# Recurrent branch: arithmetic taken from GpSimd, drive and scan a pair behind, S5 rounding and one gate moved

## The chip, the cores and the metric

One core of one Trainium2 chip. The metric is device time in microseconds of one execution. Its engines are named here as in the profile: PE (TensorE's products) and PEld (its weight loads), DVE (VectorE), ACT (ScalarE), POOL (GpSimd), SP (SyncE, which only issues DMA here; ScalarE issues some too). The kernel before takes 1066.37 us, the median of 3 runs (1065.94 to 1066.80).

## The reference, cut to what matters

One layer of a backbone over 128 prompt and 512 sample tokens of 1024 channels, in fp32. `hn` is the normed and modulated input. Two branches come from it and are merged by sigmoid gates; an FFN follows.

```python
z = hn @ p["w_in"]
xa, ga, xs = split(z)                       # 1024, 1024 and 512 channels
u  = dwconv(xa, conv_w, conv_b)             # width 4 along the tokens
for d in (forward, backward):               # the recurrent branch (RG-LRU)
    r, i = sigmoid(u @ w_r[d] + b_r[d]), sigmoid(u @ w_i[d] + b_i[d])   # blocks of 64 channels
    log_a = -8 * r * softplus(-lambda[d])
    h[d] = scan(a = exp(log_a), b = sqrt(-expm1(2 * log_a)) * (i * u))
ya = gelu(ga) * (h[0] + h[1])
vs = gelu(S5(xs) + d * xs);  ys = vs * sigmoid(vs @ s5_w_glu + s5_b_glu)
gate_a, gate_b = split(sigmoid(hn @ w_gate + b_gate))
m  = (gate_a * (ya @ w_proj_lru) + gate_b * (ys @ w_proj_s5)) @ w_out
x  = x + g1 * rmsnorm(m);  then the FFN
```

## The kernel before

**Tiles.** Channels lie on partitions, tokens along the free axis, so a tile is 128 channels by 640 tokens, or by 644 to 648 where the prompt and the sample have borders for the convolution. The 1024 channels of the recurrent branch are 8 chunks `c`.

**Precision.** Every fp32 operand of a product is split in two halves of type fp32r: `hi` is the operand rounded, `lo` what is left, and a product is hi by hi, lo by hi and hi by lo. So each operand needs a rounding and a subtraction ahead of TensorE. For weights, `split_next` (L124) takes the next of the list `units`: ScalarE rounds `raw` to `wh`, VectorE subtracts to `wl`. The list is also the order in which SP loads the 512 KB of a unit, into four `raw` buffers; a load can start when the fourth unit before it is split. `use` (L153) makes a unit and, with `ahead=2`, the two behind it ready. For activations the pairs are `uh`, `ul` (from `u`, the convolution's output), `vsh`, `vsl` (from the S5 output `vs`), `ysh`, `ysl` (from the gated S5 output `yf`), and `yah`, `yal` (from a finished chunk of the branch).

**Order.** Nothing is scheduled by a planner: each engine executes its instructions in the order in which the code writes them, and waits on others by semaphores. PSUM has four buffers of one output tile each, so a product needs that the fourth tile before it has been read. SBUF tiles come from two pools, `tp` (20 tiles) and `lp` (27).

**The S5 end.** The last of four `vs` tiles is made by GELUs in `y_out` (L1019); a loop over `ct` (L1205) splits them, and `glu_job` (L1214) multiplies with `w_glu`, takes the sigmoid and multiplies with `vs`.

**The recurrent branch** is written as functions of a chunk: `lru_xa` (product), `lru_x` (copy of the product out of PSUM with a bias, borders set by GpSimd), `lru_conv` (four passes of VectorE and the rounding `uh`), `lru_ul`, `lru_w` (split of the small block weights), `lru_gates` (four products r and i of both directions, their sigmoids on ScalarE, `i` times `u` on GpSimd), `lru_ga` and `lru_gelu` (the GELU gate), `lru_decay` (tanh, exp and sqrt of a pair of chunks on ScalarE, a table load ahead of each kind), `lru_drive` (on VectorE (1 + a) times `ta`, on GpSimd times i·u; called the driving term below), `lru_scan` (two directions of prompt and sample, 128 and 512 columns each; two copies of the final state and the sum of directions on GpSimd) and `lru_finish` (times the GELU, split into `yah`, `yal`). The sigmoid's table is loaded ahead by `warm`.

The loop at L1231 goes over the pairs c = 2, 4, 6. A pass projects and convolves the chunks c and c+1, makes gates, decay and driving terms of c-2 and c-1, and scans and finishes c-4 and c-3. The last pass also rounds the S5 output `ys`. Behind the loop (L1281 on) come the gates of chunks 6 and 7, the scans 4 and 5, the last GELUs, decay, driving terms and scans of 6 and 7, and eight `ps5_job`s: the product of `ys` with `w_proj_s5`, and on VectorE its product with a mixing gate. The 16 mixing gates were made early (`gate_job`, L762) and all but one written to DRAM (`gd`); `gate_load` (L1267) reads such a gate tile back with a DMA that is issued from ScalarE's queue (`gld`). The 16th is made here, behind scan 7. Then q_pl, the eight products of `ya` with `w_proj_lru` (L1337 on), needs all eight `yah`, `yal`, and the output projection and the FFN follow.

## Time and profile before

| | |
|---|---|
| median of 3 runs | 1066.37 us (1065.94 to 1066.80) |
| the profiled execution, its own time | 1066.57 us |
| its span, first to last instruction | 1064.8 us |
| PE busy | 1001.6 us, 94% |
| PEld busy | 917.2 us, 86% |
| DVE busy | 714.2 us, 67% |
| ACT busy | 441.0 us, 41% |
| POOL busy | 301.1 us, 28% |
| bytes moved by DMA | 124.92 MB |
| chain that ended last, by engine | PE 66%, DVE 27%, issue 3%, DMA 2%, ACT 2% |

The shares are averages over stages with different limits. The S5 end runs until about 319 us, the recurrent branch from there to 488.83, where the first q_pl product starts; the projections and the FFN take the rest. Matmuls are pipelined with modelled ends, so a busy PE is not PE at its peak.

### The profile page before, as it was taken

Reading aid. Unit: us, or ns where it says so; the run is one execution under the profiler, and the core shown is the slowest. Engines: PE = TensorE matmul, PEld = TensorE weight load, DVE = VectorE, ACT = ScalarE, POOL = GpSimd, SP = SyncE. Lnnn points to the kernel's source line nnn. Section 1 sums busy time; section 2 is a strip of 40 time slices with the busy share of each in tenths; the row PEclk is TensorE's granted clock in tenths of the full one; section 3 lists DMA queues with packets and bytes.
Section 4 is the critical chain, followed back from the end, with each engine's and each line's share of the span. In section 5 each row is a group of like instructions: output and inputs, shape, how many; then the busy total and the mean of one; then the engine's idle time right before and its main releaser. Section 6 shows DMA issues by size and latency. Waiting matters only on the chain.

```text
span 1064.8 us, 16738 instructions
## 1 busy us (share of the span) xinstructions
PE 1001.6 (94%) x6615; PEld 917.2 (86%) x6615; DVE 714.2 (67%) x1127; ACT 441.0 (41%) x704; POOL 301.1 (28%) x248
## 2 busy tenths in 40 slices
PE   5998999989999998689999996999999999999997
PEld 3697888889999888588888886999999999888885
DVE  5689999983489999996346687555565565444114
ACT  5533332324439566741133325444444445333112
POOL 4000000000016665841220094555555452000002
PEclk9899999989999998899999998999999999999999
DMA  9774268624212220345656222232223332531202
GB/s 308 239 177 109 78 172 244 196 86 123 61 43 77 60 70 21 106 141 183 200 208 214 86 80 60 81 92 87 80 80 87 93 95 91 193 117 60 79 20 99
DMA packets 137134, 124.92 MB, mean 117 GB/s; under 512 B 17272, under 2 KB 115848, under 8 KB 137056
## 3 DMA queue, kind: packets, MB, share of 16 engines
q1 hardware_dynamic: 130384, 111.82, 34.5%
q10 hardware_dynamic: 6096, 11.90, 3.3%
q8 instruction: 52, 0.85, 0.3%
q0 software_dynamic: 576, 0.13, 0.1%
q14 instruction: 26, 0.21, 0.1%
HBM read 111.31 MB, written 12.53 MB: 116 GB/s over the span
## 4 chain that ended last, share of the span: by engine, by line
PE 66%; DVE 27%; issue 3%; DMA 2%; ACT 2%; SPq 0%; DVEq 0%; ACTq 0%
PE f L65 14%; PE ffX L65 13%; PE ffY L65 7%; PE q_pl L65 5%; PE q_wo L65 5%; PE q_ga L65 4%; DVE wl L59 3%; PE ffZ L65 3%; DVE F L59 3%; DVE hh L1156 3%; DVE sc L59 3%; PE q_g L65 2%; PE q_xa L65 2%; PE q_y L65 2%; PE q_xs L65 2%
## 5 line engine op out<-in xcount | busy, mean ns | idle before, releaser
L59 DVE TENSOR_TENSOR wl<-raw,wh 128x1024 fp32r<-128x1024 f32 x100 | 129.7, 1304 | 118.1 <-ACT wh L62 118.1
L62 ACT ACTIVATE wh<-raw 128x1024 fp32r<-128x1024 f32 x104 | 109.0, 1055 | 171.7 <-PE f L65 81.8
L59 DVE TENSOR_TENSOR wl<-s,wh 128x1024 fp32r<-128x1024 f32 x40 | 58.2, 1456 | 61.6 <-ACT wh L62 61.6
L65 PE MATMUL f<-wh,al 128*128 128x512 f32 x220 | 87.0, 396 | 0.0
L65 PE MATMUL f<-wl,ah 128*128 128x512 f32 x220 | 87.0, 396 | 0.0
L65 PE MATMUL f<-wh,ah 128*128 128x512 f32 x220 | 87.0, 395 | 0.0
L59 POOL TENSOR_TENSOR s<-raw 128x512 f32<-128x512 f32 x40 | 55.8, 1396 | 56.0 <-DVE wl L59 29.6
L997 POOL MEMSET Hst<- 128x8 f32 x4 | 0.4, 111 | 233.1 <-DMA Kd<-kt 181.7
L65 PE MATMUL q_g<-hnh,wh 128*128 128x320 f32 (+1 forms) x256 | 61.8, 323 | 3.1 <-DVE modT L59 3.1
L65 PE MATMUL q_g<-hnl,wh 128*128 128x320 f32 (+1 forms) x256 | 60.2, 317 | 0.0
L65 PE MATMUL q_g<-hnh,wl 128*128 128x320 f32 (+1 forms) x256 | 59.6, 315 | 0.0
L65 PEld LDWEIGHTS q_g<-hnh,wh 128*128 128x128 f32 x256 | 44.1, 196 | 8.5 <-ACT shift L62 5.0
L65 PEld LDWEIGHTS f<-wh,al 128*128 128x128 f32 x220 | 41.4, 188 | 9.9
L65 PEld LDWEIGHTS f<-wh,ah 128*128 128x128 f32 x220 | 41.4, 188 | 9.9
L65 PEld LDWEIGHTS f<-wl,ah 128*128 128x128 f32 x220 | 41.4, 188 | 9.9
L65 PE MATMUL ffX<-Th,wh 128*128 128x320 f32 x160 | 49.4, 309 | 0.0
L65 PE MATMUL ffX<-Th,wl 128*128 128x320 f32 x160 | 49.4, 309 | 0.0
L65 PE MATMUL ffX<-Tl,wh 128*128 128x320 f32 x160 | 49.4, 309 | 0.0
L59 POOL TENSOR_TENSOR x1b<-fo,x1b 128x512 f32<-128x512 f32 x4 | 6.9, 1722 | 149.2 <-DVE fo L1685 149.2
L62 ACT ACTIVATE u<-ffX 128x320 f32<-128x320 f32 x40 | 17.5, 437 | 67.6 <-PE ffX L65 67.6
L65 PEld LDWEIGHTS q_g<-hnl,wh 128*128 128x128 f32 x256 | 44.6, 195 | 0.0
L65 PEld LDWEIGHTS q_g<-hnh,wl 128*128 128x128 f32 x256 | 44.5, 194 | 0.0
(380 smaller groups left out, 3008.2 us busy)
## 6 DMA issues: line engine op xcount, KB each, us to landing
raw<-in_w_ff_in SPq DMA_DIRECT2D x44, 512.0 KB
raw<-in_w_mod SPq DMA_DIRECT2D x32, 512.0 KB
raw<-in_w_ff_out SPq DMA_DIRECT2D x22, 512.0 KB
raw<-in_w_in SPq DMA_DIRECT2D x20, 512.0 KB
wm<-in_w_mod SPq DMA_DIRECT2D x16, 512.0 KB
raw<-in_w_gate SPq DMA_DIRECT2D x16, 512.0 KB
gd<-gate ACTq DMA_DIRECT2D x15, 320.0 KB
gld<-gd ACTq DMA_DIRECT2D x15, 320.0 KB
```

The costliest lines, as they stand in the source:

```text
L59: (eng or DVE).tensor_tensor(out=out, in0=a, in1=b, op=op)
L62: ACT.activation(out=out, in_=in_, func=func, **kw)
L65: PE.matmul(out, lhsT=lhsT, rhs=rhs, start=start, stop=stop, skip_group_check=True)
L997: POOL.memset(hv[:, :, :, 16:17], 0.0)
L1156: DVE.tensor_tensor_scan(out=ov, data0=av, data1=bv, initial=ini, op0=ALU.mult, op1=ALU.add)
```

## The change

- **GpSimd's arithmetic.** In the recurrent branch and behind it, all products, sums, copies and low halves of GpSimd go to VectorE: i·u (now `lru_iu`, L1122), the second factor of the driving term, the sum of directions, the state copies, `ul`, two weights' `wl` and some `yal`. GpSimd keeps the memsets of the borders, and from q_pl on the sums of the mixed branches.
- **Roundings.** The high halves `uh`, `yah`, `ysh`, `vsh` and the copies of `xa` out of PSUM go from VectorE to ScalarE.
- **Order of a pass.** Driving terms and scans of a pair run in the next pass, between its two `lru_xa`; the products i·u, the splits of `u` and of the block weights and the second `lru_ga` stand between tanh and exp (`middle`), the next weight's split between exp and sqrt. `low` holds back the subtraction of `yal`.
- **The end.** The S5 output `ys` is split behind the gates of 6 and 7. The 16th mixing gate is made ahead of all `ps5_job`s, and its weight stands ahead of all `w_proj_s5` in the list of units. The loads of gate tiles 8 to 15 are issued behind the last GELUs, which stand behind the decay of 6 and 7.

`lru_decay(cs, between, then)`, unchanged, calls `between` behind tanh and `then` behind exp.

```diff
+    U_G.append(unit(colmajor(w_gate, GO[15] * 128), (128, KD, 128)))
     U_PS = [unit(w_ps5[:, m * 256:m * 256 + 256].rearrange("(k p) c -> p k c", p=128), (128, 4, 256))
-            for m in range(2)]
-    U_G.append(unit(colmajor(w_gate, GO[15] * 128), (128, KD, 128)))
-    U_PS += [unit(w_ps5[:, m * 256:m * 256 + 256].rearrange("(k p) c -> p k c", p=128), (128, 4, 256))
-             for m in range(2, 4)]
...
-        b = shift(q, eng=DVE)
-        DVE.tensor_scalar(out=x[:, 2:130], in0=q[:, 192:320], scalar1=b[:, 0:1], scalar2=None, op0=ALU.add)
-        DVE.tensor_scalar(out=x[:, 133:645], in0=q[:, 320:832], scalar1=b[:, 1:2], scalar2=None, op0=ALU.add)
+        b = shift(q)
+        act(x[:, 2:130], q[:, 192:320], AF.Identity, bias=b[:, 0:1])
+        act(x[:, 133:645], q[:, 320:832], AF.Identity, bias=b[:, 1:2])
-        cw = lambda k: vec("conv_w", k * 8 + c)
-        DVE.tensor_scalar(out=u, in0=x[:, 0:644], scalar1=cw(0), scalar2=vec("conv_b", c),
+        DVE.tensor_scalar(out=u, in0=x[:, 0:644], scalar1=vec("conv_w", c), scalar2=vec("conv_b", c),
-            DVE.scalar_tensor_tensor(out=u, in0=x[:, k:k + 644], scalar=cw(k), in1=u, op0=ALU.mult, op1=ALU.add)
+            DVE.scalar_tensor_tensor(out=u, in0=x[:, k:k + 644], scalar=vec("conv_w", k * 8 + c), in1=u,
+                                     op0=ALU.mult, op1=ALU.add)
+        fr[c] = (u,)
+
+    def lru_ul(c):
+        u = fr[c][0]
-        DVE.tensor_copy(out=uh, in_=u)
-        fr[c] = (u, uh, ul)
-
-    def lru_ul(c):
-        u, uh, ul = fr[c][0:3]
-        tt(ul, u, uh, ALU.subtract, POOL)
+        act(uh, u, AF.Copy)
+        tt(ul, u, uh, ALU.subtract)
+        fr[c] += (uh, ul)
...
     def lru_gates(c):
-        u, uh, ul, wh, wl = fr.pop(c)
+        u, uh, ul, wh, wl = fr[c]
...
+
+    def lru_iu(c):
+        u = fr.pop(c)[0]
+        for d in range(2):
+            tt(bk[c][d, 1], bk[c][d, 1], u, ALU.mult)
 
     def lru_decay(cs, between=None, then=None):
 
...
-    def lru_drive(ta, cs, eng=None):
+    def lru_drive(ta, cs):
-                tt(bk[c][d, 1], bk[c][d, 1], t, ALU.mult, eng or POOL)
-
-    def lru_scan(c, eng=None):
+                tt(bk[c][d, 1], bk[c][d, 1], t, ALU.mult)
+
+    def lru_scan(c):
...
-        (eng or POOL).tensor_copy(out=nl[:, 0, c:c + 1], in_=h[0][:, NP - 1:NP])
-        (eng or POOL).tensor_copy(out=nl[:, 1, c:c + 1], in_=h[1][:, 0:1])
+        DVE.tensor_copy(out=nl[:, 0, c:c + 1], in_=h[0][:, NP - 1:NP])
+        DVE.tensor_copy(out=nl[:, 1, c:c + 1], in_=h[1][:, 0:1])
-        tt(hf, hf, hb, ALU.add, eng or POOL)
+        tt(hf, hf, hb, ALU.add)
-    def lru_finish(c, eng=None):
+    def lru_finish(c):
+
-        DVE.tensor_copy(out=yh, in_=hf)
-        tt(yl, hf, yh, ALU.subtract, eng)
+        act(yh, hf, AF.Copy)
+        lows.append(lambda: tt(yl, hf, yh, ALU.subtract))
...
-        DVE.tensor_copy(out=vh, in_=v[:, 0:T])
+        act(vh, v[:, 0:T], AF.Copy)
...
+    ta = None
     for c in range(2, 8, 2):
-        xq = [lru_xa(c)]
-        if c > 2:
+        q = lru_xa(c)
+        if ta:
+            lru_drive(ta, (c - 4, c - 3))
             lru_scan(c - 4)
+        xs = [lru_x(c, q)]
+        q = lru_xa(c + 1)
+        if ta:
             lru_scan(c - 3)
-        xq.append(lru_xa(c + 1))
-        xs = [lru_x(c + j, xq[j]) for j in range(2)]
-        for j in range(2):
-            lru_conv(c + j, xs[j])
-            if c > 2:
-                lru_finish(c - 4 + j)
-        for j in range(2):
-            lru_gates(c - 2 + j)
-        for j in range(2):
-            lru_ul(c + j)
-            lru_w(c + j)
-        gq = [lru_ga(c), lru_ga(c + 1, ahead=1)]
-        ta = lru_decay((c - 2, c - 1))
-        lru_drive(ta, (c - 2, c - 1))
-        if c == 6:
-            use(U_PS[0], 0)
-            for m, g in enumerate(yf):
-                yh = ttile(f"ysh{m}", dt=F32R)[:, 0:T]
-                yl = ttile(f"ysl{m}", dt=F32R)[:, 0:T]
-                DVE.tensor_copy(out=yh, in_=g)
-                tt(yl, g, yh, ALU.subtract)
-                ys.append((yh, yl))
+        lru_conv(c, xs[0])
+        xs.append(lru_x(c + 1, q))
+        lru_gates(c - 2)
+        lru_gates(c - 1)
+        lru_conv(c + 1, xs[1])
+        gq = [lru_ga(c)]
+
+        def middle():
+            lru_iu(c - 2)
+            lru_iu(c - 1)
+            for j in range(2):
+                lru_ul(c + j)
+            for j in range(2):
+                lru_w(c + j)
+            gq.append(lru_ga(c + 1, ahead=1))
+
+        ta = lru_decay((c - 2, c - 1), middle, split_next)
+        if c == 4:
+            lru_finish(c - 4)
+            lru_finish(c - 3)
+            low()
         if c < 6:
             for j in range(2):
                 lru_gelu(c + j, gq[j])
...
+    gate_t[7] = gate_job(15, lp)
+    lru_drive(ta, (4, 5))
+    lru_iu(6)
+    lru_iu(7)
+    for m, g in enumerate(yf):
+        yh = ttile(f"ysh{m}", dt=F32R)[:, 0:T]
+        yl = ttile(f"ysl{m}", dt=F32R)[:, 0:T]
+        act(yh, g, AF.Copy)
+        tt(yl, g, yh, ALU.subtract)
+        ys.append((yh, yl))
     lru_scan(4)
+    ta = lru_decay((6, 7), lambda: [split_next(), lru_finish(2), lru_finish(3), low()])
     lru_scan(5)
     for j in range(2):
         lru_gelu(6 + j, gq[j])
-    split_next()
-    for m in range(8, 15):
+    for m in range(8, 16):
         gate_load(m, tp)
-    ta = lru_decay((6, 7), split_next, lambda: split_next(lo_eng=POOL))
+    ps5(0)
     for m in range(2):
         gate_load(m, lp)
-    ps5(0)
+    lru_drive(ta, (6,))
+    lru_scan(6)
+    ps5(1)
     lru_finish(4)
-    ps5(1)
+    ps5(2)
+    lru_drive(ta, (7,))
+    lru_scan(7)
     lru_finish(5)
-    lru_drive(ta, (6,), DVE)
-    lru_drive(ta, (7,))
-    split_next(lo_eng=POOL)
-    ps5(2)
-    lru_scan(6, DVE)
-    gate_load(15, tp)
+    low()
+    ps5(3)
     for m in range(2, 4):
         gate_load(m, lp)
-    ps5(3)
-    lru_finish(6, POOL)
-    lru_scan(7, DVE)
-    gate_t[7] = gate_job(15, lp)
+    lru_finish(6)
     ps5(4)
     lru_finish(7)
+    low()
     ps5(5)
     ps5(6)
     ps5(7)
```

How the engines' rows stand now is shown at three places. A row is the line, the operation, its output and inputs (numbers tell buffers of one name apart) and its shape; behind "Now", lines are those of the changed file.

**First place: ScalarE, pass c = 2, from the last tanh of chunks 0 and 1 to their first exp.** `ta` is tanh's output, `ri` the gate r that becomes a, `sp` the softplus table, `u` the convolution of chunks 2 and 3, `lw0`, `lw1` their block weights. Before:

```order
L62 ACTIVATE ta_3751<-ri_3594,sp_491 128x644
L62 ACTIVATE ta_3753<-ri_3613,sp_491 128x644
L62 ACT_TABLE_LOAD
L62 ACTIVATE ri_3556<-ri_3556,sp_491 128x644
L62 ACTIVATE ri_3575<-ri_3575,sp_491 128x644
```

Now:

```order
L62 ACTIVATE ta_3674<-ri_3581,sp_491 128x644
L62 ACTIVATE ta_3676<-ri_3599,sp_491 128x644
L62 ACTIVATE uh_3682<-u_3525 128x644
L62 ACTIVATE uh_3686<-u_3610 128x644
L62 ACTIVATE lwh_3690<-lw0_3194 128x512
L62 ACTIVATE lwh_3698<-lw1_3200 128x512
L62 ACT_TABLE_LOAD
L62 ACTIVATE ri_3545<-ri_3545,sp_491 128x644
```

The two roundings of `u` and the two of the block weights stand between tanh and exp; before, the first were VectorE's and the second stood elsewhere on ScalarE.

**Second place: VectorE at the head of pass c = 4, the driving terms of chunks 0 and 1.** `wl` from `raw` is the low half of a weight; `wh_3782` is the high half of the weight of `lru_ga(4)`. Before:

```order
L59 TENSOR_TENSOR wl_3645<-raw_3227,wh_3644 128x1024
L1144 SCALAR_TENSOR_TENSOR ta_3747<-ri_3556,ta_3747 128x644
L1144 SCALAR_TENSOR_TENSOR ta_3749<-ri_3575,ta_3749 128x644
L1144 SCALAR_TENSOR_TENSOR ta_3751<-ri_3594,ta_3751 128x644
L1144 SCALAR_TENSOR_TENSOR ta_3753<-ri_3613,ta_3753 128x644
L59 TENSOR_TENSOR wl_3785<-raw_3298,wh_3784 128x1024
```

Now:

```order
L59 TENSOR_TENSOR lwl_3691<-lw0_3194,lwh_3690 128x512
L59 TENSOR_TENSOR lwl_3699<-lw1_3200,lwh_3698 128x512
L59 TENSOR_TENSOR wl_3760<-raw_3298,wh_3759 128x1024
L59 TENSOR_TENSOR wl_3783<-raw_3412,wh_3782 128x1024
L1152 SCALAR_TENSOR_TENSOR ta_3670<-ri_3545,ta_3670 128x644
L59 TENSOR_TENSOR ri_3554<-ri_3554,ta_3670 128x644
L1152 SCALAR_TENSOR_TENSOR ta_3672<-ri_3563,ta_3672 128x644
L59 TENSOR_TENSOR ri_3572<-ri_3572,ta_3672 128x644
```

And ScalarE now, from its last sqrt of that pair (`ta`) over both GELUs (`gel`) to that weight:

```order
L62 ACTIVATE ta_3676<-ta_3676 128x644
L62 ACTIVATE shift_3770<-q_ga_3615 128x2
L62 ACT_TABLE_LOAD
L62 ACTIVATE gel_3769<-q_ga_3615,shift_3770 128x128
L62 ACTIVATE gel_3769<-q_ga_3615,shift_3770 128x512
L62 ACTIVATE shift_3775<-q_ga_3706 128x2
L62 ACTIVATE gel_3774<-q_ga_3706,shift_3775 128x128
L62 ACTIVATE gel_3774<-q_ga_3706,shift_3775 128x512
L62 ACT_TABLE_LOAD
L62 ACTIVATE warm_3779<-halfpi_79 128x1
L62 ACTIVATE wh_3782<-raw_3412 128x1024
```

Ahead of the driving terms now stands one more weight, whose high half ScalarE makes behind both GELUs; each driving term is followed by its product on VectorE.

**Third place: ScalarE behind the last sigmoid of the gates of chunks 6 and 7.** `gld` is a gate tile read back, `gate` the 16th mixing gate. Before:

```order
L62 ACTIVATE ri_4674<-q_gl_4667,V_202 128x644
L62 ACTIVATE shift_4696<-q_ga_4455 128x2
L62 ACT_TABLE_LOAD
L62 ACTIVATE gel_4695<-q_ga_4455,shift_4696 128x128
L62 ACTIVATE gel_4695<-q_ga_4455,shift_4696 128x512
L62 ACTIVATE shift_4701<-q_ga_4510 128x2
L62 ACTIVATE gel_4700<-q_ga_4510,shift_4701 128x128
L62 ACTIVATE gel_4700<-q_ga_4510,shift_4701 128x512
L62 ACTIVATE wh_4705<-raw_4198 128x1024
L1267 DMA gld_4711<-gd_893 128x640
L1267 DMA gld_4713<-gd_893 128x640
```

Now, the head and, behind the four tanh, four exp and four sqrt that follow it, the end:

```order
L62 ACTIVATE ri_4643<-q_gl_4636,V_202 128x644
L62 ACTIVATE wh_4646<-raw_4196 128x1024
L62 ACTIVATE shift_4701<-q_g_4645,V_202 128x2
L62 ACTIVATE gate_4700<-q_g_4645,shift_4701 128x128
L62 ACTIVATE gate_4700<-q_g_4645,shift_4701 128x512
L62 ACTIVATE ysh0_4717<-sg_3253 128x640
L62 ACTIVATE ysh1_4721<-sg_3281 128x640
L62 ACTIVATE ysh2_4725<-sg_3324 128x640
L62 ACTIVATE ysh3_4729<-sg_3352 128x640
L62 ACTIVATE ta_4742<-ri_4580,sp_491 128x644
```

```order
L62 ACTIVATE ta_4748<-ta_4748 128x644
L62 ACTIVATE shift_4784<-q_ga_4425 128x2
L62 ACT_TABLE_LOAD
L62 ACTIVATE gel_4783<-q_ga_4425,shift_4784 128x128
L62 ACTIVATE gel_4783<-q_ga_4425,shift_4784 128x512
L62 ACTIVATE shift_4789<-q_ga_4508 128x2
L62 ACTIVATE gel_4788<-q_ga_4508,shift_4789 128x128
L62 ACTIVATE gel_4788<-q_ga_4508,shift_4789 128x512
L1280 DMA gld_4793<-gd_893 128x640
```

The last mixing gate, the S5 roundings and the whole decay of chunks 6 and 7 moved ahead of the two GELUs and so ahead of the gate tiles' loads.

## Rows read from the trace of the kernel before

**Rows 1.** Stretches: span, then busy PE, PEld, DVE, ACT, POOL; PEclk, DMA, GB/s

```profile
319.00:488.83 169.83, 147.75 (x913) 142.44 (x911) 164.09 (x161) 104.24 (x140) 102.06 (x69) 0.93 0.26 78
488.83:554.05 65.22, 65.22 (x442) 57.91 (x443) 26.32 (x28) 13.80 (x16) 14.01 (x7) 1.00 0.67 218
```

**Rows 2.** Chain of waits at the first q_pl: start us, us, engine, tile, line

```profile
487.86 0.83 DVE gld L59
...
488.83 7.29 PE q_pl L65 x48
```

**Rows 3.** VectorE by shape, 319.55 to 488.83: busy us, mean ns | idle

```profile
L1156 DVE TENSOR_TENSOR_SCAN hh<-ri,h 128x512 f32<-128x512 f32 x16 | 26.6, 1663 | 0.0
...
L1144 DVE SCALAR_TENSOR_TENSOR ta<-ri,ta 128x644 f32<-128x644 f32 x16 | 20.6, 1340 | 1.3 <-ACT ta L62 1.3
```

**Rows 4.** Order of time, VectorE: start us, us, operation

```profile
351.28 1.26 DVE L1156 TENSOR_TENSOR_SCAN hh<-ri,h 128x512 f32<-128x512 f32 x1
352.45 0.40 DVE L1156 TENSOR_TENSOR_SCAN hh<-ri 128x128 f32<-128x128 f32 x1
352.77 2.58 DVE L1156 TENSOR_TENSOR_SCAN hh<-ri,h 128x512 f32<-128x512 f32 x1
```

**Rows 5.** Order of time, GpSimd

```profile
352.71 1.56 POOL L59 TENSOR_TENSOR hh<-hh 128x640 f32<-128x640 f32 x1 [0.19 <-DVE hh L1156]
```

**Rows 6.** Order of time, VectorE; in brackets idle before and its releaser

```profile
298.06 0.61 DVE L1068 TENSOR_SCALAR u<-xap,V 128x644 f32<-128x644 f32 x1
298.71 2.75 DVE L1071 SCALAR_TENSOR_TENSOR u<-xap,V,u 128x644 f32<-128x644 f32 x3
...
317.20 2.35 DVE L59 TENSOR_TENSOR wl<-raw,wh 128x1024 fp32r<-128x1024 f32 x2
...
338.53 5.82 DVE L1144 SCALAR_TENSOR_TENSOR ta<-ri,ta 128x644 f32<-128x644 f32 x4 [0.24 <-ACT ta L62]
...
466.37 1.56 DVE L1144 SCALAR_TENSOR_TENSOR ta<-ri,ta 128x644 f32<-128x644 f32 x2
...
475.68 0.12 DVE L1157 COPY nl<-hh 128x1 f32<-128x1 f32 x1
```

**Rows 7.** ScalarE by shape, 285 to 560

```profile
L62 ACT ACTIVATE mh<-gld 128x640 fp32r<-128x640 f32 x8 | 5.9, 735 | 12.0 <-POOL gld L59 12.0
```

**Rows 8.** Order of time, ScalarE

```profile
329.13 3.00 ACT L62 ACTIVATE ta<-ri,sp 128x644 f32<-128x644 f32 x4
...
345.20 1.99 ACT L62 ACTIVATE wh<-raw 128x1024 fp32r<-128x1024 f32 x2
...
418.55 0.84 ACT L62 ACTIVATE ta<-ri,sp 128x644 f32<-128x644 f32 x1 [3.28 <-DVE u L1071]
419.41 1.28 ACT L62 ACT_TABLE_LOAD   x1
...
427.66 1.28 ACT L62 ACT_TABLE_LOAD   x1
429.06 1.47 ACT L62 ACTIVATE ri<-q_gl,V 128x644 f32<-128x644 f32 x2
...
435.31 1.70 ACT L62 ACTIVATE ri<-q_gl,V 128x644 f32<-128x644 f32 x2 [0.35 <-PE q_gl L65]
...
439.69 0.68 ACT L62 ACTIVATE gel<-q_ga,shift 128x512 f32<-128x512 f32 x1
```

**Rows 9.** Order of time, ScalarE, the last GELU of the S5 branch

```profile
290.34 0.94 ACT L62 ACTIVATE gel<-q_ga,shift 128x128 f32<-128x128 f32 x2
```

**Rows 10.** Chain of waits: TensorE's products of one output

```profile
289.38 7.08 PE q_glu L65 x48
...
320.81 5.60 PE q_gl L65 x36
...
359.22 7.12 PE q_gl L65 x36
```

**Rows 11.** Chain of waits: one gate tile written to DRAM

```profile
113.70 2.04 DMA gd<-gate
```

More of the change, by code (lines that the diff above doesn't have):

```diff
@@ L220, in hybrid_step_kernel @@
                          for m in range(2)]
+    U_G.append(unit(colmajor(w_gate, GO[15] * 128), (128, KD, 128)))
     U_PS = [unit(w_ps5[:, m * 256:m * 256 + 256].rearrange("(k p) c -> p k c", p=128), (128, 4, 256))
-            for m in range(2)]
-    U_G.append(unit(colmajor(w_gate, GO[15] * 128), (128, KD, 128)))
-    U_PS += [unit(w_ps5[:, m * 256:m * 256 + 256].rearrange("(k p) c -> p k c", p=128), (128, 4, 256))
-             for m in range(2, 4)]
+            for m in range(4)]
     U_PL, U_WO = [], []
@@ L1032, in y_out, with low @@
         vs.append(v)
+    lows = []
+    def low():
+        while lows:
+            lows.pop(0)()
     lw = []
@@ L1114, in lru_gates @@
             r[d, i] = t
-            if i:
-                tt(t, t, u, ALU.mult, POOL)
         bk[c] = r
+    def lru_iu(c):
+        u = fr.pop(c)[0]
+        for d in range(2):
+            tt(bk[c][d, 1], bk[c][d, 1], u, ALU.mult)
     def lru_decay(cs, between=None, then=None):
```

## The prediction

> **What bounds the kernel now.** I read the stretches first. Between 319.0 and 488.8 us, the recurrent branch, VectorE is busy 164.1 us of 169.8 and TensorE 147.8; from 488.8 on, TensorE is busy without a gap for 65.2 us [rows 1]. So this change is decided by when the first q_pl product starts, 488.83, and a later start is a later end, because no idle time of TensorE follows in which it could be made up for 65 us. The chain of waits shows what releases q_pl: VectorE's product of a gate tile with a PSUM result of S5, which frees the buffer [rows 2]. The groups of VectorE show why it is so full: its 16 scans of 512 columns take 1.66 us on the mean and the 16 multiply-adds on `ta` 1.34 [rows 3], but in the order of time one scan takes 1.26 and a later one of the same shape 2.58 [rows 4], the latter while GpSimd adds two scans [rows 5]. VectorE pays for GpSimd's arithmetic in its own time.
>
> The Trainium skill explains this (SBUF — State Buffer, "Who interferes with whom"): an operation of VectorE with two SBUF inputs and one of GpSimd that reads SBUF exclude each other for a whole instruction. The trace agrees, 1.26 against 2.58 us. By that the change gives every remaining operation of VectorE its short time.
>
> **Prices.** From VectorE rows without GpSimd beside them [rows 4, 6]: one direction of a scan is 0.32 + 1.17, so 3.0 for a chunk of both directions; the state copies 0.1 and the sum of directions one pass of 0.8, together 3.9. A pass over 644 columns takes 0.8 (1.56 for two of the driving terms), so a driving term with its product 1.6 and the four of a pair 6.4. A convolution is 0.65 + 2.75 = 3.4. The low half of a weight (`wl`) is 1.15 (2.35 for two). ScalarE rounds 640 columns in 0.74 [rows 7] and a weight in 1.0 [rows 8]; no row shows `u`, `hf` or the S5 tiles there, and I take 0.74 for each, between 0.65 back to back and 1.0 as for 1024 columns.
>
> The gain that the change aims at: GpSimd's passes now cost VectorE 0.8 each, but everything on VectorE takes its short time and the rounding leaves it. Its own work in the stretch comes to 8 x (3.2 + 3.9 + four passes 3.2) + 6 x (3.4 + two passes 1.6) + 17 weights x 1.15 + 4 S5 and 6 gate passes 8.0 = 140 us, 30 less than the stretch. That is not the time, because ScalarE and VectorE now wait for each other in their written orders. I follow them.
>
> **S5 rounding on ScalarE.** `vsh` now stands behind the last GELU, which begins at 290.34 and ends at 291.3 [rows 9]; + 0.74 + a VectorE pass 0.83 it is 292.9 before the first glu product has both halves. It began at 289.38 [rows 10]. Lag 3.5 us. TensorE's 36 equal gate products took 5.60 after one stop and 7.12 after another [rows 10], so up to 1.5 more; against that, the wait before 320.81 for VectorE's copies of xa falls away. I take 3 at the end of the first gates, between 2 and 5.
>
> **The passes over pairs.** Before, ScalarE's four tanh began at 329.13 and ended at 332.13, and the weight rounding after the GELUs ended at 346.2 (345.20 + 1.0): 14.1 us for exp, sqrt, two GELUs, four table loads and one rounding [rows 8]. The driving terms began at 338.53 [rows 6], as soon as the square roots ended. Now VectorE's order has the low half of GA4 ahead of the driving terms, and its high half stands behind both GELUs on ScalarE (second place of the order above). So they wait: 332.1 + 3 + two roundings of `u` 1.4 + 14.1 + one more weight 1.0 + 1.15 = 352.8, against 338.5. This is the step that I hold decisive. That an engine does not pass by a waiting instruction is in the rows: ScalarE's tanh at 418.55 stood 3.28 us behind VectorE's `u`, while the table load behind it had nothing to wait for [rows 8]. The Trainium skill says the same (Perfetto Trace Analysis, "Tensor Engine Instruction"): ScalarE and VectorE are strict FIFOs. If VectorE could pass the weight by, the driving terms would start where the square roots end, 345.8, and each of the first two passes would be 7 us shorter.
>
> The pass is a loop of both engines, since exp stands behind the rounding of both `u` (first place). VectorE: driving terms 6.4 + scan 3.9 + weight 1.15 + scan 3.9 + two convolutions 6.8 = 22.1. ScalarE: last `u` 0.75 + two gate weights 1.0 + 14.1 + one more weight 1.0 + two `ya` 1.4 = 18.3. VectorE: weight 1.15. Together 41.6, so the second driving terms start at 394.4. The third pass has no GELU: 22.1 + 0.75 + 1.0 + 1.0 and from the table load of exp to the sigmoid of gates 6 and 7 9.65 (419.41 to 429.06) makes 429.0, and their eight sigmoids, which TensorE feeds through two free PSUM buffers because both q_ga are still held, end 7.95 later as they did (429.06 to 437.01) [rows 8]: 437.0. That is where they ended before. So at the last gates nothing is won or lost; but VectorE has the driving terms of chunks 4 and 5 still before it, and before the change it had not.
>
> **Behind the last gates.** ScalarE rounds the second S5 weight at 438.0, VectorE its low half at 439.2 (again ahead of the driving terms). Driving 6.4, four passes 3.2, S5 low halves 3.2: 452.0. The mixing gate's product and sigmoid and the four `ysh` are done by 447 beside this. The third tanh needs the tile that the first direction of scan 4 reads: 453.5, fourth tanh 455.0, weight 1.0, low half 457.2, two products 1.6, `yah3` 0.74: 459.5. Then table load, exp, table load, sqrt 8.2 (419.41 to 427.66) and the two GELUs with their load 3.4 (437.01 to 440.37) [rows 8]: 471.1. Only now are the gate tiles asked for (third place); 320 KB the other way took 2.04 us [rows 11], so the first is there at about 473.5, at least 471.5. VectorE is done with scan 5 at 464.5 and stands in front of the product with that tile for 9 us. Behind it are driving term 6 and all that follows: six gate products 4.8, driving 6.4, two scans 7.8, four products 3.2, four low halves 3.2, two weights 2.3, and twice a rounding of `ya` plus a weight on ScalarE that VectorE waits for 3.6: 31.3 us. 473.5 + 31.3 = 504.8, q_pl at 505.0 instead of 488.8.
>
> **Sum.** 16.2 us. S5's first weights and U_G15 change places on SP's queue, ahead of their use by four buffers: nothing, hidden behind the third pass; without that cover one transfer of 512 KB, about 3 by the 2.04 us for 320 KB [rows 11]. Of the ten gate tiles that ScalarE's queue now asks for late only the first is waited for: the second is used 8 us behind it. GpSimd's memsets of the borders have nothing behind them that another engine waits for early. The profiled execution took 1066.57 (span 1064.8), 0.2 above the median 1066.37; 1066.4 + 16.2 = **1082.6 us**. Bounds: lag 2 to 5, gate tile 471.5 to 474.5, roundings 0.65 to 1.0 at some 20 places of which 8 lie on the path, and 1.5 for each of two cold starts of TensorE before q_pl: 1077 to 1090.
>
> **Rivals.** (a) *The busy time decides.* If the waits at the head of the passes did not bind, the stretch would shrink to VectorE's 140 or TensorE's 148 us, by 22 to 30, less the lag of 3: about 1043, faster by 2%. For it: VectorE is 97% busy now. Against it: VectorE stands still until the GELUs are over; the rival needs the low half of GA4 done before 346, which its place forbids. The Trainium skill (Perfetto Trace Analysis, "Optimizing Scalar/DVE Operations") says that moving work to ScalarE may make sense if VectorE is saturated; by that the change wins, and it is this rival. I give it 0.10, and 0.05 to half of it, which with the wait for the gate tile ends within 2 us. (b) *The gate tile is early.* ScalarE's queue issues the loads ahead of its arithmetic and the 9 us and part of the 3.6 vanish: 488.8 + 16.2 - 12 gives 1070. For it: before, loads were issued between GELUs; against: the wait of the GELU for its shift holds the queue. 0.10. (c) *The long times stay*, because something other than GpSimd makes them: 16 x 0.4 for the scans and 16 x 0.5 for `ta` on a path twice as tied, over 1097. Nothing in the rows speaks for it. 0.04. The forecast, 1077 to 1090, has 0.71.
>
> **Numbers.** A measurement of this kernel tells 0.2% (2 us) from no change. Faster is (a), 0.10; same is its half, 0.05; slower are the forecast, (b) and (c), 0.85. The range takes the forecast's bounds and (b): 1069 to 1090, 0.81 in all; the time is that of the forecast.
>
> **What would show it.** No arithmetic of GpSimd in the stretch and all scans at 1.25 us; VectorE idle for 8 us or more before the first and third driving terms with ScalarE's weight as releaser, and 7 to 10 us before the first gate product with a DMA or ScalarE as releaser; driving terms 42 us apart; q_pl near 505 and everything behind it moved as a block. It is wrong if VectorE is 95% busy over the stretch, if driving terms start before 346, or if q_pl starts before 495.

## The result and the profile after

| | before | changed |
|---|---|---|
| median | 1066.15 us (4 runs, 1062.90 to 1066.80) | 1080.63 us (4 runs, 1079.09 to 1084.21) |
| ratio of the runs | 1 | 1.0147, 95% interval 1.0119 to 1.0174 |
| profiled execution, its span | 1066.57, 1064.8 us | 1084.21, 1082.4 us |
| DVE, ACT, POOL busy | 714.2, 441.0, 301.1 us | 676.5, 462.8, 195.8 us |
| first q_pl product starts at | 488.83 us | 506.06 us |

The change costs 14.5 us by the medians and 17.6 between the two profiled executions (the changed one was the slowest of its four). In the trace all of it lies ahead of q_pl: 506.06 - 488.83 = 17.2 us, and from q_pl to the end it is 576.3 us against 576.0. The stretches, with the columns of [rows 1]:

```profile
319.00:506.06 187.06, 152.30 (x953) 147.78 (x951) 138.16 (x200) 120.86 (x174) 0.50 (x9) 0.90 0.23 71
506.06:571.28 65.22, 65.22 (x443) 57.93 (x444) 26.42 (x29) 13.85 (x16) 13.92 (x7) 1.00 0.66 218
```

GpSimd's 102 us are gone, VectorE fell from 164.1 to 138.2 busy, ScalarE rose from 104 to 121, and yet the stretch is 17 us longer: VectorE now stands still for 49 of 187 us. Its groups by shape show both sides, the short times against [rows 3] and the wait at the weights' low halves:

```profile
L59 DVE TENSOR_TENSOR wl<-raw,wh 128x1024 fp32r<-128x1024 f32 x17 | 20.7, 1222 | 36.4 <-ACT wh L62 36.4
L1164 DVE TENSOR_TENSOR_SCAN hh<-ri,h 128x512 f32<-128x512 f32 x16 | 20.1, 1259 | 0.0
...
L1152 DVE SCALAR_TENSOR_TENSOR ta<-ri,ta 128x644 f32<-128x644 f32 x16 | 13.2, 822 | 0.0
```

In the order of time, VectorE stands still ahead of the first driving terms (8.60 us), ahead of those of chunks 4 and 5 (14.42), and ahead of the first product with a gate tile (8.22); the time in brackets is the idle time, and behind it what ended it:

```profile
352.92 1.22 DVE L59 TENSOR_TENSOR wl<-raw,wh 128x1024 fp32r<-128x1024 f32 x1 [8.60 <-ACT wh L62]
354.06 0.82 DVE L1152 SCALAR_TENSOR_TENSOR ta<-ri,ta 128x644 f32<-128x644 f32 x1
...
440.50 1.23 DVE L59 TENSOR_TENSOR wl<-raw,wh 128x1024 fp32r<-128x1024 f32 x1 [14.42 <-ACT wh L62]
...
475.05 0.82 DVE L59 TENSOR_TENSOR gld<-q_p,gld 128x640 f32<-128x640 f32 x1 [8.22 <-DMA gld<-gd]
```

And ScalarE stands still where it did not before, between tanh and exp, until VectorE has made a convolution `u` (pass c = 4):

```profile
368.15 2.99 ACT L62 ACTIVATE ta<-ri,sp 128x644 f32<-128x644 f32 x4
372.92 0.74 ACT L62 ACTIVATE uh<-u 128x644 fp32r<-128x644 f32 x1 [1.78 <-DVE u L1074]
376.29 0.74 ACT L62 ACTIVATE uh<-u 128x644 fp32r<-128x644 f32 x1 [2.62 <-DVE u L1074]
376.94 1.14 ACT L62 ACTIVATE lwh<-lw 128x512 fp32r<-128x512 f32 x2
378.10 1.28 ACT L62 ACT_TABLE_LOAD   x1
```

At the end of the chain of waits stand the late load of the first gate tile and, as before [rows 2], a gate tile's product that releases q_pl:

```profile
472.25 2.70 DMA gld<-gd
475.05 0.82 DVE gld L59
...
505.09 0.83 DVE gld L59
506.06 7.28 PE q_pl L65 x48
```

### The profile page after: what moved, and what is told of

It reads as the page before. It is cut to its first block, busy times and chain, and to the rows that moved or that the text cites. A ratio compares the mean times of both kernels' runs of the same rounds, so it can differ in the third digit from the quotient of the medians.

```text
span 1082.4 us, 16706 instructions
## 1 busy us (share of the span) xinstructions
PE 1002.8 (93%) x6615; PEld 918.6 (85%) x6615; DVE 676.5 (63%) x1138; ACT 462.8 (43%) x751; POOL 195.8 (18%) x189
## 4 chain that ended last, share of the span: by engine, by line
PE 61%; DVE 23%; ACT 8%; DMA 4%; issue 3%; SPq 1%; DVEq 0%; ACTq 0%
PE f L65 14%; PE ffX L65 13%; PE ffY L65 6%; PE q_pl L65 5%; PE ffZ L65 3%; DVE F L59 3%; PE q_wo L65 3%; DVE wl L59 3%; PE q_xa L65 3%; DVE sc L59 3%; PE q_g L65 2%; PE q_y L65 2%; ACT L62 2%; PE q_glu L65 2%; DVE pab L59 2%
## 5 line engine op out<-in xcount | busy, mean ns | idle before, releaser
L59 DVE TENSOR_TENSOR wl<-raw,wh 128x1024 fp32r<-128x1024 f32 x102 | 127.5, 1255 | 152.5 <-ACT wh L62 152.4
L59 POOL TENSOR_TENSOR gld<-gld 128x640 f32<-128x640 f32 x7 | 13.9, 1989 | 163.5 <-DMA raw<-in_w_mod 125.3
L62 ACT ACTIVATE wh<-s 128x1024 fp32r<-128x1024 f32 x40 | 41.9, 1047 | 2.8 <-PE q_ff L65 2.8
```

The costliest lines, as they stand in the source:

```text
L59: (eng or DVE).tensor_tensor(out=out, in0=a, in1=b, op=op)
L62: ACT.activation(out=out, in_=in_, func=func, **kw)
```

## The experiments

Each run is timed beside the kernel before. Differences "against the changed kernel" are taken between ratios, with 1 us for 0.094%; the changed kernel, run once more, gives 1.0141. With intervals of some 0.2% on either side, such a difference is uncertain by some 3 us.

| run | edit | median, us | ratio to before, interval |
|---|---|---|---|
| c_changed | the changed kernel again | 1080.68 | 1.0141 (1.0118 to 1.0164) |
| e1_drive_loop | driving terms ahead of the low half, in the passes | 1072.11 | 1.0069 (1.0049 to 1.0089) |
| e2_drive_end | the same for chunks 4 and 5 | 1079.95 | 1.0137 (1.0116 to 1.0157) |
| e3_vsh | `vsh` back on VectorE | 1076.96 | 1.0111 (1.0091 to 1.0132) |
| e4_loads | two gate tiles loaded earlier | 1075.37 | 1.0094 (1.0073 to 1.0115) |
| e5_all | e1 to e4 together | 1058.68 | 0.9927 (0.9903 to 0.9951) |
| e8_more | e5, and more of the end reordered | 1052.26 | 0.9872 (0.9849 to 0.9895) |
| e11_round_back | all four roundings back on VectorE | 1062.52 | 0.9971 (0.9961 to 0.9982) |
| e7_after_pool | changed order, arithmetic back on GpSimd | 1109.33 | 1.0409 (1.0391 to 1.0427) |
| e6_before_pool | before, GpSimd's arithmetic on VectorE | 1053.44 | 0.9883 (0.9860 to 0.9905) |
| e9_pool_round | e6, `uh`, `vsh`, `ysh` on ScalarE | 1066.02 | 1.0008 (0.9997 to 1.0020) |
| e10_pool_xa | e6, copies of xa on ScalarE | 1045.02 | 0.9812 (0.9796 to 0.9827) |

**Each wait of the forecast by itself, e1 to e4.**

```diff
+        if ta:
+            lru_drive(ta, (c - 4, c - 3))
         q = lru_xa(c)
         if ta:
-            lru_drive(ta, (c - 4, c - 3))
             lru_scan(c - 4)
```

> The changed kernel with one thing moved: in the passes c = 4 and 6 the driving terms stand ahead of lru_xa, so ahead of the weight's low half whose high half ScalarE makes behind both GELUs. Theory (VectorE stands in front of that low half): the driving terms of pass 4 start at the end of the square roots, about 347 instead of 354.1; exp of that pass then is bound by the sigmoids and comes 4 us earlier, exp of pass 6 about 11 us earlier, and q_pl starts near 495 instead of 506. Time about 11 us below the changed kernel: 1069 (1065 to 1073). Rival 1 (the delay by a pair costs the time by itself, wherever the low half stands): q_pl moves by less than 3 us, time 1078 to 1081. Rival 2 (TensorE's lower clock behind its stops bounds the stretch): TensorE has no idle time left between 345 and 420 and the gain is under 5 us.

It gave 7.7 us of the 11 expected. VectorE's order of time:

```profile
343.91 0.83 DVE L1152 SCALAR_TENSOR_TENSOR ta<-ri,ta 128x644 f32<-128x644 f32 x1 [0.83 <-ACT ta L62]
...
351.68 1.23 DVE L59 TENSOR_TENSOR wl<-raw,wh 128x1024 fp32r<-128x1024 f32 x1 [1.27 <-ACT wh L62]
```

The driving terms start with the square roots, the 8.6 us in front of the low half are 1.3, and q_pl starts at 496.03. So the low half in front of the driving terms does cost time, and the delay by a pair alone does not explain the loss.

```diff
+    lru_drive(ta, (4, 5))
     gate_t[7] = gate_job(15, lp)
-    lru_drive(ta, (4, 5))
```

> The changed kernel with the driving terms of chunks 4 and 5 ahead of the 16th gate's job, so ahead of its weight's low half; the passes stay. Theory: they run beside TensorE's last gates, from about 429 to 435, instead of 441.6 to 448.1. Then the S5 roundings and the 16th gate on ScalarE, done at 449.8, bound scan 4, which starts at about 450.7 instead of 454: 3 us, time 1077.5 (1075 to 1079.5). Were VectorE's queue the only limit there, it would be 6.5 us: 1074. Rival (only TensorE's product of the 16th gate counts): no gain, 1080.6.

Inconclusive by the time: 0.4 us, and the intervals overlap. In the trace the step goes as the theory says, scan 4 starting at 449.44 behind the `ysl` that wait for the S5 roundings, and q_pl at 501.69:

```profile
446.50 3.03 DVE L59 TENSOR_TENSOR ysl<-sg,ysh 128x640 fp32r<-128x640 f32 x4 [3.31 <-ACT ysh L62]
449.44 0.42 DVE L1164 TENSOR_TENSOR_SCAN hh<-ri 128x128 f32<-128x128 f32 x1
```

But from q_pl on this execution took 575.6 us where the changed kernel's second profile took 573.0. The profiled executions differ there by up to 4.5 us (572.9 to 577.4), even those of one kernel (576.3 and 573.0 for the changed one). By the traces most of it lies in TensorE's idle time in the 135 us that begin 65 us behind the start of q_pl (9.6 to 11.7 us) and in one wait ahead of the products `ffX` (1.0 us, or 2.3 to 2.8); the cause was not studied.

```diff
-        act(vh, v[:, 0:T], AF.Copy)
+        DVE.tensor_copy(out=vh, in_=v[:, 0:T])
```

> The changed kernel with the four vsh roundings back on VectorE. Theory: the first q_glu starts at about 289.4 instead of 292.1, TensorE is not stopped there and keeps its short products (the 96 products of q_glu took 17.3 us instead of 14.1), the first tanh of the branch is at 329 instead of 332.5, and all that follows moves with it: 3.5 to 6 us, time 1076 (1074 to 1078). Rival (the lag is taken up by waits in the passes, as TensorE's stops behind 423): under 1.5 us.

It gave 3.2 us, about as much as such a difference is uncertain by; the trace has q_pl 3.3 earlier than the changed kernel's second profile (501.97 against 505.26). In the changed kernel the first glu products, on TensorE in the order of time, the stretch from 289.4 to 309.4 and its part behind the stop (columns of [rows 1]) read

```profile
292.11 0.90 PE L65 MATMUL q_glu<-vsh,wh 128*128 128x320 f32 x2 [2.58 <-ACT vsh L62]
...
289.40:309.40 20.00, 17.42 (x100) 16.94 (x99) 10.12 (x13) 10.16 (x16) 0.17 (x3) 0.83 0.12 34
292.20:298.00 5.80, 5.80 (x21) 5.44 (x22) 4.05 (x5) 3.96 (x5) 0.00 (x0) 0.50 0.07 20
```

and in e3

```profile
289.45 0.54 PE L65 MATMUL q_glu<-vsh,wh 128*128 128x320 f32 x2
...
289.40:309.40 20.00, 20.00 (x140) 20.00 (x139) 14.46 (x18) 8.72 (x13) 0.17 (x3) 1.00 0.22 62
```

The stop of 2.58 us costs TensorE more than itself: behind it the granted clock is 0.50 for some 6 us, the lower of the two levels (1.2 GHz), a pair of products takes 0.73 to 0.90 instead of 0.46, and the clock of these 20 us is 0.83 instead of 1.00. The 96 products of q_glu take 17.3 us instead of 14.1, in the changed kernel's second profile, with the same stop, 16.5. Not all of it reaches the end: the first tanh starts 4.9 us earlier in e3 than in that second profile (326.85 against 331.70), q_pl 3.3.

```diff
-    ta = lru_decay((6, 7), lambda: [split_next(), lru_finish(2), lru_finish(3), low()])
+    ta = lru_decay((6, 7), lambda: [split_next(), lru_finish(2), lru_finish(3), low(),
+                                            gate_load(8, tp), gate_load(9, tp)])
...
-    for m in range(8, 16):
+    for m in range(10, 16):
```

> The changed kernel with the loads of the gate tiles 8 and 9 issued between the last tanh and exp of chunks 6 and 7 instead of behind the last GELUs. Theory: the first gate product no longer waits 8.2 us for its tile and runs at about 467; driving term 6 then waits for the square roots, about 470.5 instead of 475.8; the two issues cost ScalarE up to 1 us: 5 us, time 1075.5 (1073.5 to 1077). Rival (the S5 product 2 waits for a PSUM buffer that the last GELUs hold, so the end of the chain is not the first tile but the GELUs): under 2 us.

It gave 5.0 us; VectorE uses the first tile at once and then waits for the square roots:

```profile
466.26 0.82 DVE L59 TENSOR_TENSOR gld<-q_p,gld 128x640 f32<-128x640 f32 x1
467.60 0.83 DVE L1152 SCALAR_TENSOR_TENSOR ta<-ri,ta 128x644 f32<-128x644 f32 x1 [0.52 <-ACT ta L62]
```

**Together, and the changed kernel again.**

> The changed kernel once more, beside the others of this group, so that they can be set against it on the same chip. All theories: 1.2 to 1.7% above the kernel before, about 1080.

> The edits of e1 to e4 together. Theory (four waits one behind the other on one path, so that the gains add): 8 from the passes, 1 to 3 from the driving terms at the end, 4 from vsh, 5.5 from the two loads: 18.5 to 20.5 below the changed kernel, 1060 (1057 to 1063), so faster than before by 0.3 to 0.4%. Rival (the gains overlap, since each frees the path to the same next wait, TensorE's gates of 6 and 7 or the 16th gate): half of it, 1070.

e5 is 22.8 us below the changed kernel, and the four single runs add up to 16.3, a sum of four uncertain differences. The traces are clearer: q_pl starts at 480.28, 25.0 us earlier than in the changed kernel's second profile (505.26), and the four edits alone moved it by 9.2, 3.6, 3.3 and 6.7, together 22.8. The waits stand behind one another on one path, and the rival, that the gains overlap and leave half, falls.

e8 goes on from e5 at the end (against e5; the lines that go behind the roundings `ysh` are not shown):

```diff
     lru_drive(ta, (4, 5))
-    gate_t[7] = gate_job(15, lp)
+    lru_scan(4)
+    lru_scan(5)
+    q = psq("q_g")
+    mtile(q, wblocks(U_G[15]), hn, range(KD))
...
+    g = ttile("gate", pool=lp)
+    seg_act(g, q, AF.Sigmoid, shift(q, vec("b_gate", GO[15])))
+    gate_t[7] = g[:, 0:T]
+    ta = lru_decay((6, 7), lambda: [lru_finish(2), lru_finish(3), gate_load(8, tp), gate_load(9, tp),
+                                    split_next(), low()])
```

> A version meant to beat both: e5, and behind the passes scans 4 and 5 ahead of the 16th gate's weight, the S5 roundings ahead of that gate's sigmoid on ScalarE, and the products of chunks 2 and 3 ahead of the next weight. Theory: the last two tanh no longer wait for scan 4, exp of 6 and 7 comes some 6 us earlier than in e5 and driving term 6 with it: 1054 (1050 to 1058). Rival (VectorE's work behind the last gates, or TensorE, bounds the end whatever ScalarE does): as e5, 1060.

It beats both kernels, by 1.3% and 2.7%, without any edit of where the work runs but `vsh`.

**One part of the change alone, from the kernel before.** e6 moves GpSimd's arithmetic to VectorE and nothing else:

```diff
-                tt(t, t, u, ALU.mult, POOL)
+                tt(t, t, u, ALU.mult)
...
-                tt(bk[c][d, 1], bk[c][d, 1], t, ALU.mult, eng or POOL)
+                tt(bk[c][d, 1], bk[c][d, 1], t, ALU.mult)
...
-        tt(hf, hf, hb, ALU.add, eng or POOL)
+        tt(hf, hf, hb, ALU.add)
```

and likewise `ul`, the state copies, two `wl` and one `yal`.

> The kernel before with one part of the change alone: GpSimd's products, sums, copies and low halves of the branch go to VectorE, in the old order, and the roundings stay on VectorE. Theory (VectorE pays for GpSimd's arithmetic in its own time): its rows of the stretch 319 to 488.8 at their short prices are 48 us less, and the operations that come to it are 40 us more, so it is some 8 us less busy and as nearly full as before: faster by 0 to 8, 1060 (1056 to 1066). All 512-column scans take 1.26. Rival (the engines only share a port at times, and two engines do more than one): VectorE is busier by up to 40 us and the time 1080 or more.

It is faster by 1.17%, 12.5 us, beyond the range. The stretch up to q_pl (columns of [rows 1]), and VectorE's groups by shape in it:

```profile
319.00:476.00 157.00, 142.59 (x924) 138.51 (x924) 148.47 (x218) 104.86 (x141) 0.43 (x9) 0.97 0.29 85
```

```profile
L1156 DVE TENSOR_TENSOR_SCAN hh<-ri,h 128x512 f32<-128x512 f32 x16 | 20.1, 1258 | 0.0
...
L1144 DVE SCALAR_TENSOR_TENSOR ta<-ri,ta 128x644 f32<-128x644 f32 x16 | 13.1, 822 | 2.2 <-ACT ta L62 2.2
...
L59 DVE TENSOR_TENSOR yal<-hh,yah 128x640 fp32r<-128x640 f32 x8 | 6.6, 825 | 0.3
...
L1168 DVE CAST yah<-hh 128x640 fp32r<-128x640 f32 x8 | 4.0, 494 | 0.3
```

and in the kernel before, the same rounding in the stretch, and one of the S5 end:

```profile
L1168 DVE CAST yah<-hh 128x640 fp32r<-128x640 f32 x8 | 11.1, 1390 | 0.3
...
290.29 0.49 DVE L1209 CAST vsh<-vs 128x640 fp32r<-128x640 f32 x1 [0.67 <-ACT vs L62]
```

VectorE takes over all of GpSimd's passes and is yet 16 us less busy (148.5 against 164.1). What I had not priced is the last row of e6: a rounding takes VectorE 0.49 us when GpSimd is still, and took 1.39 on the mean in the same place before; the 18 roundings of the stretch (`uh`, `yah`, `ysh`) take 8.9 us instead of 24.0. The price stood in the trace of the kernel before: its four `vsh`, with GpSimd still, take 0.43 to 0.49. ScalarE takes 0.74 [rows 7].

e7 is the counterpart in the new order: the same operations but the two `wl` and the `yal` go back to GpSimd (the edit of e6 turned round, on the changed file).

> The changed kernel, in its order and with its roundings on ScalarE, but with i times u, the second factor of the driving terms, the sum of directions, the state copies and ul back on GpSimd. Theory (GpSimd's arithmetic is paid by VectorE in either order, and here it also stands in series between driving term, scan and convolution): VectorE's scans and multiply-adds return to 1.3 to 2.6, GpSimd's products of 1.8 to 2.1 are waited for: 12 to 25 above the changed kernel, 1097 (1090 to 1106). Rival (the new order alone makes the loss, and where the arithmetic runs does not matter): 1080.

Slower by 28.5 us than the changed kernel, beyond the range again. VectorE's groups:

```profile
L1074 DVE SCALAR_TENSOR_TENSOR u<-xap,V,u 128x644 f32<-128x644 f32 x18 | 32.3, 1794 | 1.1
L1164 DVE TENSOR_TENSOR_SCAN hh<-ri,h 128x512 f32<-128x512 f32 x16 | 23.9, 1491 | 0.0
L59 DVE TENSOR_TENSOR wl<-raw,wh 128x1024 fp32r<-128x1024 f32 x17 | 21.1, 1245 | 43.5 <-ACT wh L62 43.5
```

The convolution's multiply-adds take twice the 0.89 that they take in e6, and the wait for the high halves grows too. In both orders GpSimd's arithmetic costs more than VectorE's. In e7 not all of it is VectorE's long times: GpSimd's own products take 2.0 us each there and stand in series between driving term and scan (VectorE waits 2.9 us for them).

**The roundings.** From e6, three of the four kinds go to ScalarE:

```diff
-        DVE.tensor_copy(out=uh, in_=u)
...
+        act(uh, u, AF.Copy)
         tt(ul, u, uh, ALU.subtract)
...
-        DVE.tensor_copy(out=vh, in_=v[:, 0:T])
+        act(vh, v[:, 0:T], AF.Copy)
...
-                DVE.tensor_copy(out=yh, in_=g)
+                act(yh, g, AF.Copy)
```

> e6 (GpSimd's arithmetic on VectorE, old order) with the roundings uh, vsh and ysh on ScalarE as in the change; uh stands with ul behind the gates. Theory: a rounding takes VectorE 0.50 and ScalarE 0.74, so VectorE wins 7 us that it partly cannot use, vsh costs 3.8 as in e3, uh puts 1.4 per pass between the sigmoids and tanh: 3 to 6 above e6, 1058 (1055 to 1060). Rival (VectorE's busy time decides): 4 to 7 below e6, 1047.

A miss: 13.3 us above e6, where 3 to 6 were expected, and all that GpSimd's removal had won. By the traces 5.9 are there at the first driving terms (344.68 against 338.82), 1.7 and 2.0 come in the two passes, and 4.5 behind the third driving terms, where ScalarE's order reads

```profile
374.87 0.74 ACT L62 ACTIVATE uh<-u 128x644 fp32r<-128x644 f32 x1 [0.84 <-DVE u L1071]
...
429.78 2.60 ACT L62 ACTIVATE ysh<-sg 128x640 fp32r<-128x640 f32 x4
...
436.66 0.80 ACT L62 ACTIVATE ri<-q_gl,V 128x644 f32<-128x644 f32 x1 [1.38 <-PE q_gl L65]
```

The first driving terms in e6 and in e9, and TensorE's wait at the last gates in e6 and in e9:

```profile
338.82 0.83 DVE L1144 SCALAR_TENSOR_TENSOR ta<-ri,ta 128x644 f32<-128x644 f32 x1 [2.19 <-ACT ta L62]
344.68 0.83 DVE L1144 SCALAR_TENSOR_TENSOR ta<-ri,ta 128x644 f32<-128x644 f32 x1 [4.77 <-ACT ta L62]
...
420.77 0.56 PE L65 MATMUL q_gl<-uh,lwh 128*128 128x322 f32 x2 [0.18 <-ACT ri L62]
434.64 0.91 PE L65 MATMUL q_gl<-uh,lwh 128*128 128x322 f32 x2 [6.12 <-ACT ri L62]
```

In e9 the four `ysh` stand ahead of the last gates' sigmoids, TensorE waits 6.12 us once for a sigmoid to free a PSUM buffer (0.18 in e6), and then feeds them slowly, with pairs of 0.74 to 0.91. This last part is not one of the changed kernel's, whose `ysh` stand behind those sigmoids.

The same question in the new order, from the changed kernel:

```diff
-        act(yh, hf, AF.Copy)
+        DVE.tensor_copy(out=yh, in_=hf)
```

and likewise `vsh`, `ysh`, and `uh` at the end of `lru_conv`.

> The changed kernel in its order, GpSimd without arithmetic, with the four kinds of rounding (vsh, uh, yah, ysh) back on VectorE; the copies of xa stay on ScalarE. Theory (a rounding on ScalarE ahead of exp ties ScalarE to VectorE's convolution of the next pair, and TensorE to the last GELU at the S5 end): vsh gives 3.5 to 4; exp of pass 4 no longer stands behind the second uh and starts at about 369 instead of 378, the driving terms of pass 6 5 us earlier, exp of pass 6 earlier by 13, the end of the last gates by 8 and more, of which VectorE gives back 3 for its own roundings; the waits for yah at the end go: 14 below the changed kernel, 1066 (1062 to 1070). Rival (the low half in front of the driving terms and the late loads are the whole loss, the roundings cost only vsh's lag): 1076.

18.1 us below the changed kernel, more than the 14 expected, and 0.3% faster than before. ScalarE goes from tanh to exp without a stop:

```profile
361.84 2.99 ACT L62 ACTIVATE ta<-ri,sp 128x644 f32<-128x644 f32 x4
364.73 1.14 ACT L62 ACTIVATE lwh<-lw 128x512 fp32r<-128x512 f32 x2
365.89 1.28 ACT L62 ACT_TABLE_LOAD   x1
```

From the first tanh to exp's table load it is 4.1 us, in the changed kernel 10.0. Of the four kinds of rounding only `vsh` was run by itself (e3); how the rest divides over `uh`, `yah` and `ysh` is not shown. That run still has the low half in front of the driving terms, and VectorE waits 8.6 us there; e1's edit on top of it was not tried.

**The copies of xa.** The part of the change that does fit, from e6:

```diff
-        b = shift(q, eng=DVE)
...
+        b = shift(q)
+        act(x[:, 2:130], q[:, 192:320], AF.Identity, bias=b[:, 0:1])
+        act(x[:, 133:645], q[:, 320:832], AF.Identity, bias=b[:, 1:2])
```

> e6 with one more part of the change, the copies of xa out of PSUM on ScalarE, in the old order. Theory: in e6 VectorE is busy 148 of the 157 us and ScalarE idle for 7.3 us ahead of the first sigmoid of a pass; the copies cost VectorE 2.5 per pass and fit that idle time: up to 7.5 below e6, 1047 (1045 to 1051). Rival (TensorE or ScalarE takes over as the bound of the pass at once): 1052 to 1054.

7.6 us below e6 and 1.9% below the kernel before, the fastest of all. Its stretch up to q_pl:

```profile
319.00:468.00 149.00, 140.89 (x921) 138.48 (x923) 139.70 (x197) 109.52 (x155) 0.43 (x9) 0.97 0.29 86
```

TensorE and VectorE are now both within 10 us of the stretch, so by these busy times moving work between engines can win little more there.

## Why the prediction was right, and where it was not

1082.6 was forecast, 1080.63 measured, within the range and with the right sign. The mechanism was right too: the two engines wait for each other at the places it named, and e1, e3 and e4 take such waits out. That q_pl came within 1.1 us is in part luck, as the points below the table show. Its stations, against the profiled execution:

| station | forecast | measured |
|---|---|---|
| first glu product | 292.9 | 292.11 |
| end of the first gates, later by (first tanh) | 3 | 3.4 (332.50 against 329.13) |
| driving terms, first and second | 352.8, 394.4 | 354.06, 395.54 |
| last sigmoid of gates 6 and 7 ends | 437.0 | 439.5 |
| first gate tile asked for | 471.1 | 472.25 |
| first product with it, VectorE idle before | 473.5, 9 | 475.05, 8.2 |
| from there to q_pl | 31.3 | 31.0 |
| q_pl | 505.0 | 506.06 |

- **VectorE pays for GpSimd** held. VectorE's own work in the stretch was forecast at 140 and is 138.2; e6 and e7 show the effect in both orders, and larger than I would have said. The Trainium skill (SBUF — State Buffer, "Who interferes with whom") has it as a lock for a whole instruction; 0.49 against 1.39 us for the same rounding agrees.
- **The first driving terms** came 1.3 late. The sum, 332.1 + 3 + 1.4 + 14.1 + 1.0 + 1.15, leaves out the two roundings of the block weights that stand behind those of `u`; in the trace they take 1.14 (336.66). The second driving terms are still late by 1.1.
- **"Up to 1.5 more" for TensorE's cold start** was too little at the S5 end: the products of q_glu took 3.2 longer. The 3 us at the end of the first gates came out all the same, because the rest of the change gave back 2.3 there: in e3, without the lag, the first tanh starts at 326.85, before at 329.13. How much of that is the wait for xa's copies was not tried alone. The last gates ended 2.5 late, 1.1 of it there from the first sigmoid on (430.17 against 429.06). TensorE's order of time there, and the stretch (columns of [rows 1]):

```profile
423.98 0.90 PE L65 MATMUL q_gl<-uh,lwl 128*128 128x322 f32 x2 [4.32 <-DVE lwl L59]
...
431.00 0.91 PE L65 MATMUL q_gl<-uh,lwh 128*128 128x322 f32 x2 [3.98 <-ACT ri L62]
...
424.00:472.00 48.00, 27.19 (x142) 25.36 (x142) 27.52 (x38) 32.79 (x45) 0.00 (x0) 0.75 0.11 33
```

Two stops, and behind each of them pairs of products at 0.90, then 0.74 us, instead of 0.46. I had let the sigmoids set the pace, as before. From there to the loads of the gate tiles the forecast was 1.3 too long, so that q_pl is off by 1.1 only.
- **"This is the step that I hold decisive"**, the low half in front of the driving terms, failed as a ranking. It is real, 7.7 us (e1), but the four kinds of rounding together are worth 18.1 (e11). They were in my sum, as "exp stands behind the rounding of both `u`", which closes the loop of 41.6 us over both engines, and as the lag of the S5 end; I never took them out of it by themselves to see what they cost.
- **"The rounding leaves it"**, as part of the gain, was the wrong sign. I took no price for a rounding on VectorE without GpSimd, though the trace of the kernel before has it (`vsh`). It is 0.49, so 24 of them relieve VectorE by 12 us and load ScalarE with 18. The Trainium skill (VectorE: DVE Perf Modes, "Mode 2×_2P — use both read ports for one tensor") says that an operation with a single source in SBUF can use both read ports and go at twice the rate even in fp32, one with two tensors can not; the rows of e6 go that way, 0.49 for the rounding and 0.82 for a subtraction over the same 640 columns.
- **Rival (a)**, the busy time decides: not for this kernel. That e10 comes near its 1043 (1045.02), in the old order and with VectorE busy 139.7 of 149.0 us, shows only that such a time can be reached. **Rival (b)**, the gate tile is early: e4 tested its size, and not 12 but 5 us vanish, since the square roots take over at 467.6. **Rival (c)**, the long times stay: no, the 16 scans take 1.26 on the mean.

A path through the runs leads from the kernel before to the changed one and so adds up to the loss by construction: 12.5 us won by GpSimd's arithmetic (e6), 7.6 by the copies of xa (e10), 16.9 lost from e10 to e11, which differ in the order, the driving terms' place and the late loads, and 18.1 lost by the roundings. How the 16.9 divide was measured on the changed kernel (e1, e2 and e4, together 13.1), not on e11.

## What to carry to other kernels

Take GpSimd off a busy VectorE first and alone, in the old order, and only then move anything else: here that by itself won 12.5 us, and the moves made with it lost more than twice that. Before an operation goes to another engine, ask what that engine's queue must wait for at the new place, and what stands behind it: the copies of xa filled ScalarE's idle time and won 7.6 us, while roundings between tanh and exp tied two engines into one chain (10.0 us there instead of 4.1, in pass c = 4). In a written order, look for each instruction whose input is made behind a long run of another engine, and see what stands behind it.

## What was not expected of the hardware

- A rounding of 640 columns on VectorE takes 0.49 us without GpSimd beside it, 1.39 on the mean with it. The kernel before showed both, the first in its `vsh`; I had not used it.
- A stop of TensorE of 2.58 us was followed by some 6 us at the lower clock (granted 0.50), so that the 96 products of q_glu took 17.3 us instead of 14.1 (16.5 in another execution): with the stop itself 5 to 6 us at that place, of which some 3 reached q_pl.
- Behind q_pl, in work that no edit touches, executions differ by up to 4.5 us (572.9 to 577.4), 3.3 of them between two executions of one kernel.
